# Loads of y ahead of the last output gate, at the joint of attention and merge

## The chip, the core and the metric

The kernel runs on one core of a Trainium2 chip. The time is the device time of one execution in microseconds; below, every number of the trace is in microseconds from the start of the span unless it says ns.

## The reference

Two layers over 1024 tokens of width 1024, all in float32. In each layer four branches give y_a, y_b, y_c, y_m (gated MLP, sparse attention, forgetting attention, memory attention), each 512 wide and each multiplied by the silu of a projection of its own, the output gate. Then the branches are merged:

```python
y_b = nsa_attention(...) * jax.nn.silu(b_z)
up = jnp.einsum('bsnw,nwd->bsnd', ys, w_br)
gates = jax.nn.sigmoid(jnp.einsum('bsd,dne->bsne', h, w_gate))
merged = jnp.einsum('bsnd,bsnd->bsd', gates, up)
out = merged @ w_o
return x + rms_norm(out, g_post)
```

## The kernel before, in words

Every product in full precision is made of three matmuls: each operand is split into a high part (rounded, on ScalarE, `split` L328 or `weight` L220) and a low part (the rest, on VectorE, or on GpSimd for weights), and `mm3` (L247) multiplies high by high, low by high and high by low (lines 251, 254, 255 of the trace). A projection of one 128-column weight for one half of the tokens (c is 0 or 1, 512 tokens) is 8 x 3 = 24 matmuls into a PSUM bank of the pool pj (two banks).

A layer runs `gates` and `attention`, then `merge`. At the end of `attention` the sparse attention's heads are worked off in units of 256 queries (`nsa_unit` L994): scores (L601, L602), exponentials into tiles p, transposes into PSUM (pt, L633; the compressed part's from tiles pc), their eviction and split on ScalarE and VectorE (L331, L333), and the products with the values (o, L641, L645). `head_out` (L648) then adds the parts in a tile yt on ScalarE and GpSimd and stores it by SP (L657) to od, 64 rows by 256 tokens at a time. Between the scores, work that has nothing to do with them is planned to fill TensorE; its list FILL ends with gate y4, whose two tiles th are stored for later (L521). The fill follows the scores at a pace: `follow` (L261) ties a matmul to a score matmul by order alone.

`gate_out` (L1208) makes one output gate: for each half, it loads the head pair's output (tile oo, L1215), projects, takes tanh on ScalarE (z, L341) and a step on VectorE (L342), multiplies by oo on GpSimd (L1217) and stores y (L1218). The last one, bz of head pair 3 in branch 1, is the first thing in `merge`, since it needs the last head.

`add_branch` (L1300) goes over the branches in the order 0, 2, 3, 1. `get_y` (L1310) loads the branch's four tiles yf for each half and splits them into yh and yl. A unit (`gated` L1320) is then 12 matmuls into a bank of s (three banks), a tile th with the gate, and a VectorE step into acc. For branch 0 all gates have been stored before, so th is only loaded. Units of branch 0 run e = 0 to 7 and c = 0, 1.

What sets the order: instructions are ordered by a planner with a clock of its own, program order being the priority; each engine, and SP's queue of DMAs, then works in that order. Within a pool, tiles of one tag take turns in its buffers, and `order_slots` (L174) adds this: the first write of a tile waits for the first write of the tile before it of the same tag, to be complete if it is on another engine. The tag st (eight buffers of 2 KB) serves z, oo, yf and th alike. Pools of the attention lie one behind the other in SBUF: pp (p, 12 x 2 KB), qq (queries, 2 x 4), cb (also the pc tiles, 4 x 2), cd (1 KB), yt (3 x 2), and more. In `merge` the pool yh (5 x 8 KB) begins where pp began, and acc0 and acc1 (16 KB each) follow it; a tile can be written as soon as the tiles under it are done with.

Of the kernel before, what the change touches and what calls it, by code (L numbers as in the profile page):

```python
# [213 lines left out]
class Net:  # L214
# [993 lines left out]
    def gate_out(self, n, name, p):  # L1208
# [3 lines left out]
        for c in range(2):  # L1212
# [4 lines left out]
            nc.gpsimd.tensor_mul(z, z, o)  # L1217
            nc.sync.dma_start(self.y[n][p, :, cs], z)  # L1218

    def gate_early(self, n, e):  # L1220

        w = self.a_form(f"g{n}{e}")
        for c in range(2):
            t = self.st("th")
            self.gate_store(n, e, c, t, self.proj(w, c))
# [51 lines left out]
    def merge(self):  # L1277
        nc, tc, a, l = self.nc, self.tc, self.a, self.l
        p = lambda n, b: tc.tile_pool(name=n, bufs=b, reuse_waits="tile")
        with p("yh", 5) as self.pyh:  # L1280
            with p("acc", 1) as pacc:
                self.acc = [pacc.tile([128, 8, 512], F32, name=f"acc{c}") for c in range(2)]
                self.gate_out(1, "bz", 3)
                for n in (0, 2, 3, 1):
                    self.add_branch(n)
            gp = self.pyh.tile([128, 1024], F32, name="gp", tag="yh")
            nc.sync.dma_start(gp, a["g_post"][l].partition_broadcast(128))
            self.early = "banks"
            with p("kf", 4) as self.pkk, p("vf", 3) as self.pvv, p("tf", 1) as self.ptp:
                self.out_proj(0, gp)  # L1290
                if l + 1 < self.depth:
                    self.mem_norm(l + 1)
                self.out_proj(1, gp)
                if l + 1 < self.depth:
                    self.l, self.xsrc = l + 1, self.x1
                    self.fresh()
                    self.mem_kv()
                    self.prenorm()

    def add_branch(self, n):  # L1300
        yy = [self.get_y(n, c) for c in range(2)]
        for cs in ((0, 1),) if n != 1 else ((0,), (1,)):
            for e in range(8):
                wg = None if (n, e, 0) in self.ready else self.a_form(f"g{n}{e}")
                if e % 2 == 0:
                    wu = [z.rearrange("p (e w c) -> p e w c", e=2, w=4) for z in self.weight(f"u{n}{e // 2}")]
                for c in cs:
                    self.gated(n, e, c, wg, [z[:, e % 2] for z in wu], yy[c])
# [154 lines left out]
```

## Time and profile before

| | us |
|---|---|
| median of 3 runs (3148.03 to 3160.84) | 3156.19 |
| the profiled execution | 3157.73 |
| its span, first to last instruction | 3155.9 |
| TensorE busy | 3047.0 (97%) |
| VectorE busy | 1884.3 (60%) |
| ScalarE busy | 1487.9 (47%) |
| GpSimd busy | 1439.2 (46%) |
| mean granted clock of TensorE, as a share of 2.4 GHz | 0.989 |

In the views PE is TensorE, PEld its weight load, DVE VectorE, ACT ScalarE, POOL GpSimd, SP the queue that issues DMAs. Matmuls are pipelined: the duration of one is longer than its distance to the next. "x" counts instructions; "<-" names what ended an idle time.

### The profile page before, as it was taken

What the parts mean: (1) busy time and instruction counts of PE and PEld (TensorE: products, weight loads), DVE (VectorE), ACT (ScalarE), POOL (GpSimd) and SP (SyncE); (2) the same over time, 40 slices, a digit from 0 to 9 for tenths busy, and PEclk for the clock granted to TensorE, in tenths of its full rate; (3) what the DMA queues carried; (4) which work ended last, traced back from release to release, by engine and by line L of the source; (5) the groups of instructions that cost most, each with busy time, mean ns of one, the idle gap of its engine ahead of it and who ended that gap; (6) DMA issues with size and microseconds to landing.
All of it is one profiled execution on the core that took longest, in us unless ns stands there. A gap on an engine that the chain in (4) does not pass through costs nothing.

```text
span 3155.9 us, 45143 instructions
## 1 busy us (share of the span) xinstructions
PE 3047.0 (97%) x15168; PEld 2548.8 (81%) x15168; DVE 1884.3 (60%) x4313; ACT 1487.9 (47%) x3313; POOL 1439.2 (46%) x1142
## 2 busy tenths in 40 slices
PE   7999999999999999899999999999999999998998
PEld 6778878888888888688787788788878888886887
DVE  7555447868667855336474653578785678553363
ACT  5433345566556654323353433455655566552132
POOL 6844534543233322258577445355432333232684
PEclk9999999999999999999999999999999999998999
DMA  6544495564234322456665345855632342324564
GB/s 221 153 134 132 140 276 158 177 191 125 84 108 146 106 94 94 139 174 195 205 201 177 104 130 162 251 164 180 200 104 83 113 146 96 105 89 149 171 197 147
DMA packets 251673, 475.15 MB, mean 151 GB/s; under 512 B 42513, under 2 KB 96785, under 8 KB 251441
## 3 DMA queue, kind: packets, MB, share of 16 engines
q1 hardware_dynamic: 251440, 472.26, 47.6%
q8 instruction: 120, 1.97, 0.3%
q14 instruction: 113, 0.92, 0.1%
HBM read 334.73 MB, written 137.43 MB: 150 GB/s over the span
## 4 chain that ended last, share of the span: by engine, by line
PE 82%; DVE 5%; DMA 4%; POOL 3%; issue 2%; ACT 2%; SPq 1%; DVEq 0%; POOLq 0%; ACTq 0%
PE pj L251 11%; PE pj L254 11%; PE pj L255 11%; PE s L481 5%; PE s L301 5%; PE s L254 5%; PE o L645 5%; PE s L251 5%; PE s L255 5%; PE pt L633 5%; PE pj L481 4%; PE pj L301 4%; PE s L601 3%; PE s L602 3%; DVE p L674 1%
## 5 line engine op out<-in xcount | busy, mean ns | idle before, releaser
L229 POOL TENSOR_TENSOR wl<-wr,wh 128x1024 fp32r<-128x1024 f32 (+1 forms) x232 | 527.4, 2275 | 609.9 <-ACT wh L227 535.0
L251 PE MATMUL pj<-hh,wh 128*128 128x512 f32 x1648 | 651.5, 395 | 2.4 <-DVE z L342 1.8
L255 PE MATMUL pj<-hh,wl 128*128 128x512 f32 x1648 | 652.3, 396 | 0.0
L254 PE MATMUL pj<-hl,wh 128*128 128x512 f32 x1648 | 650.5, 395 | 0.0
L227 ACT ACTIVATE wh<-wr 128x1024 fp32r<-128x1024 f32 x232 | 245.5, 1058 | 341.1 <-PE s L254 86.7
L611 ACT ACTIVATE p<-p,nm 128x384 f32<-128x384 f32 (+3 forms) x512 | 306.8, 601 | 203.5 <-DVE nm L606 200.4
L333 DVE TENSOR_TENSOR pt<-pt,pt 128x512 fp32r<-128x512 f32 (+1 forms) x464 | 291.9, 635 | 134.8 <-ACT pt L331 133.4
L251 PEld LDWEIGHTS pj<-hh,wh 128*128 128x128 f32 x1648 | 310.9, 189 | 61.0 <-DVE z L342 2.7
L255 PEld LDWEIGHTS pj<-hh,wl 128*128 128x128 f32 x1648 | 310.6, 188 | 59.2
L254 PEld LDWEIGHTS pj<-hl,wh 128*128 128x128 f32 x1648 | 310.6, 188 | 58.0
L331 ACT ACTIVATE pt<-pt 128x512 fp32r<-128x512 f32 (+1 forms) x464 | 251.7, 554 | 212.5 <-PE pt L633 154.3
L645 PE MATMUL o<-pt,v 128*128 128x512 f32 (+1 forms) x864 | 245.1, 371 | 8.8 <-DVE pt L333 8.5
L654 POOL TENSOR_TENSOR yt<-yt 128x256 f32<-128x256 f32 x128 | 100.1, 782 | 300.9 <-ACT yt L653 241.0
L633 PE MATMUL pt<-ident,p 128*128 128x128 f32 x1488 | 230.6, 272 | 0.7 <-DVE pt L333 0.5
L251 PE MATMUL s<-yh,wh 128*128 128x512 f32 x512 | 201.1, 396 | 24.7 <-ACT yh L331 24.7
L633 PEld LDWEIGHTS pt<-ident,p 128*128 128x128 f32 x1488 | 184.9, 140 | 43.0 <-DVE pt L333 0.7
L254 PE MATMUL s<-yl,wh 128*128 128x512 f32 x512 | 201.4, 393 | 0.8 <-DVE yl L335 0.8
L255 PE MATMUL s<-yh,wl 128*128 128x512 f32 x512 | 200.7, 392 | 0.0
L601 PE MATMUL s<-kd,q 128*128 128x512 f32 (+2 forms) x512 | 187.4, 369 | 13.2 <-DVE nm L606 13.2
L602 PE MATMUL s<-kl,q 128*128 128x512 f32 (+2 forms) x512 | 175.5, 344 | 0.0
L645 PEld LDWEIGHTS o<-pt,v 128*128 128x128 f32 x864 | 147.6, 188 | 33.4 <-DVE pt L333 13.6
L676 DVE TENSOR_SCALAR p<-p,r,sg 128x384 f32<-128x384 f32 (+2 forms) x320 | 165.9, 574 | 1.7
(379 smaller groups left out, 6577.4 us busy)
## 6 DMA issues: line engine op xcount, KB each, us to landing
wr<-wt SPq DMA_DIRECT2D x250, 512.0 KB
th<-thd SPq DMA_DIRECT2D x124, 256.0 KB
thd<-gu SPq DMA_DIRECT2D x72, 256.0 KB
q<-rq SPq DMA_DIRECT2D x32, 512.0 KB
yf<-y SPq DMA_DIRECT2D x64, 256.0 KB
thd<-th SPq DMA_DIRECT2D x52, 256.0 KB
vd<-vs SPq DMA_DIRECT2D x48, 256.0 KB
v<-vd SPq DMA_DIRECT2D x24, 512.0 KB
```

Source lines behind the costliest of these rows:

```text
L229: nc.gpsimd.tensor_sub(lo[:, :n], raw[:, :n], hi.bitcast(F32)[:, :n])
L251: ins = nc.tensor.matmul(out, ah, bh, start=k == 0, stop=False)
L254: nc.tensor.matmul(out, ah, bl, start=False, stop=False)
L255: nc.tensor.matmul(out, al, bh, start=False, stop=k == n - 1)
L301: self.nc.tensor.matmul(ps[i], a[:, kk, ts], b[:, k], start=kk == n == 0, stop=kk == 7 and n == 2)
L333: (nc.gpsimd if pool else nc.vector).tensor_sub(lo, src, hi.bitcast(F32))
L481: nc.tensor.matmul(out, w[a][:, k], t[b][:, k], start=start and k == x == 0, stop=k == 3 and x == 2, skip_group_check=True)
L601: self.mark(nc.tensor.matmul(ps[:, :w], q[:, tq], kd[:, b0:b0 + w], start=True, stop=False), 1 + n / 128)
L602: nc.tensor.matmul(ps[:, :w], q[:, tq], kl[:, b0:b0 + w], start=False, stop=True)
L611: nc.scalar.activation(p[:, :n], p[:, :n], AF.Exp, bias=init, scale=-1.0, accum_out=l[:, x:x + 1])
L633: nc.tensor.transpose(pt[:, off + x * 128:off + x * 128 + 128], src, self.ident)
L645: nc.tensor.matmul(o[:, :, t0:t0 + m], it["v"], w[:, :, off:off + m], start=first, stop=last)
```

## The change

`gate_out` of the last gate is taken out of `merge` and cut in two. `gate_begin` loads and splits the weight, projects both halves and makes both z; it stands in `add_branch` of branch 0 behind the loads of y, and while it is traced the pace is set so that its projections come behind the last score matmul in TensorE's order. `gate_end` loads both oo, multiplies and stores; it stands ahead of e = 2 of branch 0, so behind four units.

```diff
+    def gate_begin(self, name, p):
+        w = self.a_form(f"{name}{p}")
+        zz = []
+        for c in range(2):
+            z = self.st("z")
+            self.silu2(z, self.proj(w, c))
+            zz.append(z)
+        return zz
+
+    def gate_end(self, n, p, zz):
+        for c, z in enumerate(zz):
+            cs = slice(c * 512, c * 512 + 512)
+            o = self.st("oo")
+            self.nc.sync.dma_start(o, self.od[n][p, :, cs])
+            self.nc.gpsimd.tensor_mul(z, z, o)
+            self.nc.sync.dma_start(self.y[n][p, :, cs], z)
...
                 self.acc = [pacc.tile([128, 8, 512], F32, name=f"acc{c}") for c in range(2)]
-                self.gate_out(1, "bz", 3)
                 for n in (0, 2, 3, 1):
                     self.add_branch(n)
...
         yy = [self.get_y(n, c) for c in range(2)]
+        if n == 0:
+            self.pace = (1, 1, 1, 0.0)
+            gated = self.gate_begin("bz", 3)
+            self.pace = None
         for cs in ((0, 1),) if n != 1 else ((0,), (1,)):
             for e in range(8):
+                if n == 0 and e == 2:
+                    self.gate_end(1, 3, gated)
```

## Rows read from the trace of the kernel before

**Rows 1.** The page: busy time by engine, and the chain's shares by engine.
```profile
PE 3047.0 (97%) x15168; PEld 2548.8 (81%) x15168; DVE 1884.3 (60%) x4313; ACT 1487.9 (47%) x3313; POOL 1439.2 (46%) x1142
...
PE 82%; DVE 5%; DMA 4%; POOL 3%; issue 2%; ACT 2%; SPq 1%; DVEq 0%; POOLq 0%; ACTq 0%
```

**Rows 2.** Waits of TensorE, 1270 to 1330: us in total, times, longest.
```profile
PE s L251 <- ACT yh L331: 12.1, 1, 12.1
PE o L645 <- DVE pt L333: 2.4, 5, 0.6
```

**Rows 3.** Waits of TensorE, 2838 to 2910.
```profile
PE s L251 <- ACT yh L331: 12.6, 1, 12.6
```

**Rows 4.** Windows, first layer: length, busy by engine (instructions), PEclk, DMA share, GB/s.
```profile
1263.50:1279.20 15.70, 15.69 (x79) 12.82 (x77) 7.35 (x21) 7.20 (x17) 4.07 (x4) 1.00 0.23 71
1279.20:1289.90 10.70, 8.27 (x46) 5.99 (x46) 5.50 (x9) 5.82 (x11) 5.52 (x5) 1.00 0.26 80
1289.90:1302.00 12.10, 0.01 (x1) 0.00 (x0) 0.69 (x2) 2.24 (x4) 2.70 (x3) 0.67 0.32 99
1302.00:1307.80 5.80, 5.78 (x13) 4.28 (x14) 4.30 (x7) 4.01 (x7) 0.00 (x0) 0.52 1.01 350
1307.80:1345.00 37.20, 37.20 (x165) 30.78 (x165) 10.68 (x16) 6.11 (x8) 7.18 (x3) 1.00 0.56 177
```

**Rows 5.** Windows, second layer: the gap and the stretch behind it.
```profile
2859.24:2871.85 12.61, 0.00 (x2) 0.00 (x1) 0.71 (x2) 2.26 (x5) 2.70 (x3) 0.56 0.30 97
2871.85:2877.82 5.97, 5.97 (x14) 4.42 (x14) 4.44 (x7) 4.10 (x7) 0.00 (x0) 0.51 1.02 350
```

**Rows 6.** The chain that ended last, 1292 to 1303: start, us, what.
```profile
1292.67 1.92 DMA o<-yt
1294.64 2.69 DMA oo<-o
1297.36 0.61 ACT z L341
1297.98 3.33 DMA yf<-y
1301.34 0.64 ACT yh L331
1302.02 0.79 PE s L251
```

**Rows 7.** Timeline of SP: start, us, instruction, count.
```profile
1266.34 0.32 SPq L521 DMA_DIRECT2D thd<-th  x1
...
1285.96 7.16 SPq L657 DMA_DIRECT2D o<-yt  x2
...
1297.98 2.22 SPq L1316 DMA_DIRECT2D yf<-y  x5
```

**Rows 8.** Timeline of TensorE: projections, last scores, last transposes of pc and p.
```profile
1257.01 0.50 PE L251 MATMUL pj<-hh,wh 128*128 128x512 f32 x1 [0.88 <-DVE z L342]
...
1263.12 0.34 PE L602 MATMUL s<-kl,q 128*128 128x384 f32 x1
...
1278.79 0.40 PE L255 MATMUL pj<-hh,wl 128*128 128x512 f32 x1
...
1281.09 0.27 PE L633 MATMUL pt<-ident,pc 128*128 128x128 f32 x1
...
1287.63 0.49 PE L633 MATMUL pt<-ident,p 128*128 128x128 f32 x3
```

**Rows 9.** Instructions on the tile yf: ns min/median/max, first and last start.
```profile
L335 DVE SCALAR_TENSOR_TENSOR yl<-yf,yh x64: 677/691/2859, 1302.0 to 3022.4; 128x512 fp32r<-128x512 f32 x64
```

**Rows 10.** Timeline of GpSimd in the last head's stretch.
```profile
1280.43 2.37 POOL L229 TENSOR_TENSOR wl<-wr,wh 128x1024 fp32r<-128x1024 f32 x1
```

**Rows 11.** Timelines of VectorE and GpSimd, later in the first merge.
```profile
1350.68 2.79 DVE L335 SCALAR_TENSOR_TENSOR yl<-yf,yh 128x512 fp32r<-128x512 f32 x2
...
1349.61 2.71 POOL L229 TENSOR_TENSOR wl<-wr,wh 128x1024 fp32r<-128x1024 f32 x1 [8.54 <-ACT wh L227]
```

## The prediction

> **What bounds the kernel now.** I read the page's busy shares and its chain first. TensorE is busy 97% of the span and 82% of the chain runs over it [rows 1]: work taken off another engine is worth nothing by itself, and only microseconds in which TensorE stands still, or runs at the lower clock, can be won. So the next view is TensorE's waits around the two places that the diff touches, the joints between attention and merge. The last head's second half ends on TensorE at 1289.9 us in the first layer and 2859.2 us in the second, and the first matmul of the merge, waiting for the split of a y tile, starts 12.1 and 12.6 us later [rows 2, 3]. No other single wait in the first of them is over 0.6 us [rows 2].
>
> The windows show the rest of the loss. Before the gap the granted clock is 1.00 (2.4 GHz); in the gap it falls to 0.67 and 0.56 as a mean, and in the 5.8 and 6.0 us behind it, it is 0.52 and 0.51, which is the lower level, 1.2 GHz [rows 4, 5]. Only 13 and 14 matmuls run in these two stretches. At the pace of the stretch that follows (165 in 37.20 us, 0.225 us each [rows 4]) they would take 2.9 and 3.2 us. So the lower clock and the waits for splits in it cost 2.9 us in the first layer and 2.8 in the second. The gap and its cold tail together: 12.1 + 2.9 + 12.6 + 2.8 = 30.4 us, 1.0% of the time.
>
> What fills the gap is in the chain, in order of time [rows 6]: the last store of the last head's output takes 1.92 us, the load of its half tile for the output gate (oo) 2.69, the tanh of the gate's projection (z) 0.61, and only then the first y load 3.33, its split 0.64, the first matmul of the merge. The tanh needs nothing from oo, and the y loads of branch 0 need nothing from the gate of head pair 3: y[0] was finished long before. They stand in this order because all of them take tiles of the tag st, and the first write of each such tile waits for the first write of the one before it in the program. SP's own list shows the same: the y loads go out right behind that tanh, at 1297.98 [rows 7].
>
> **The change part by part.**
>
> Moved: the 16 y loads (8 in each layer) now come ahead of the gate's z and oo in the program. The st tiles before them are the two th of y4, whose second store goes out at 1266.34 [rows 7]. With eight buffers and eight loads the last one can go when that store has read its tile, about 2 us later by the 1.92 us of the chain's store. Five of these loads were issued in 2.22 us [rows 7], so eight take 3.6; the first landed after 3.33 [rows 6], and their 2.1 MB at the 350 GB/s of the busy stretch [rows 4] take 6 us, where the DMA share is now only 0.23 to 0.26. So from 1268.3 all y tiles are in SBUF by about 1278, before the last head ends. SP passes eight more entries ahead of the head's stores; this delays a store by 3.6 us at most, and no store is on TensorE's path any more.
>
> The splits of y then need their destinations. The five 8 KB buffers of yh lie on three pieces of pp, one of qq and one of cb. qq is free after the last scores (1263.12), cb when the last transpose of a pc tile is through (1281.09), and the last p tile is read at 1287.63 [rows 8]. So the pair of half c=0 can be written from about 1281.4 on if the planner takes qq and cb, and at the worst from 1288.1, still 1.8 us before the last matmul of the head. A split takes 0.64 us on ScalarE and 0.69 on VectorE [rows 6, 9], and a unit of the merge uses one pair per three matmuls, 0.68 us: one split ahead of TensorE is enough.
>
> Held back: the 48 projection matmuls of bz3. In the trace the last scores run at 1263.12 and the projections behind them are still those of y4 [rows 8]: 72 projection matmuls run from 1257.01 to 1278.79, the first 24, to 1264.5, for y4's second half, the other 48 for bz3. Those already stand behind the last scores, so this order takes away nothing that was used. I price it at 0; it would cost up to 48 x 0.225 = 10.8 us per layer if these matmuls had filled holes before the scores, but the stretch behind the scores is full either way (15.69 of 15.70 us busy [rows 4]). The two banks of pj stay occupied until the z's are read; branch 0 has all its gates stored and asks for no pj, so nobody waits.
>
> Moved later: two oo loads, two multiplications on POOL, two stores of y[1], now ahead of the fifth unit of branch 0. Branch 1 is the last that reads them. POOL is busy 7.18 of the 37.20 us there [rows 4], and TensorE waits for none of it. 0.
>
> What is late next. The merge's first DVE result goes to acc0, which lies on the buffers of yt: it must wait for the head's last store, which lands at 1294.6 [rows 6]. TensorE has three banks of s, three units of 12 matmuls or 8.1 us, before it needs that; starting at 1289.9 it gets to 1298. The th loads wait, by the same rule of order, for the second z; a load like oo's takes 2.69 us, so z must be done by about 1294. Both covers are some 3 us.
>
> What is left to pay is crowding. In the stretch of the last head (10.70 us) VectorE is busy 5.50 [rows 4]; eight splits and one more z step of 0.69 add 6.2, 11.7 in all: 1.0 us too much. Beside it POOL subtracts a weight for 2.37 us [rows 10], and a pair of splits beside such a subtraction took 2.79 us instead of 1.38 [rows 11]: 1.4 more. So the price is between a gain of 2.4 us a layer (the holes of the last head, 10.70 less 8.27 [rows 4], filled with merge matmuls that come early) and a loss of 2.4. I take 1.5 lost, near the upper of the two: the head's own splits and these share in-order queues. The sum: 30.4 less 2 x 1.5 = 27.4 us.
>
> One rule speaks against the change. The row first: POOL's 2.71 us subtraction at 1349.61 and the two y splits at 1350.68 that end after it [rows 11]. The Trainium skill, SBUF — State Buffer, section Who interferes with whom, says that a VectorE instruction with two SBUF inputs and a GpSimd instruction that reads SBUF exclude each other for a whole instruction. By it every POOL step in the last head's stretch would hold up a split, also the small yt additions, for which no row of this trace has a split beside them; the sum would be that of the first rival below.
>
> The profiled execution took 3157.7 us (span 3155.9), 1.5 above the median of the runs, 3156.2. 3157.7 - 27.4 = 3130.3; on the scale of the median 3128.8, so 3129.
>
> **The rivals.**
>
> Crowding at its full size. The splits and z's stand in the queues of ScalarE and VectorE between the last head's evictions. That head waits already for its evictions (five waits, 2.4 us [rows 2]). For: POOL is busy 5.52 us in that stretch [rows 4], and a split beside a POOL step has waited for it [rows 11]. Against: TensorE has merge matmuls to run meanwhile, and the small steps may fall between the splits. If all of the 5.52 falls on the path, 30.4 - 2 x 5.5 = 19.4 is won: 3137.
>
> The loads don't come early. SP issues in order; if the planner puts the y loads behind the last head's two stores, they go out at about 1293.1, land 3.3 us later, and with 0.64 for the split TensorE starts at 1297.1: 4.9 us a layer won, the clock still lost. 3156.2 - 9.8 = 3146, no change by measure. For: the planner issues by its own clock, and two stores stand there for 7.16 us [rows 7]. Against: the loads' tiles are free 17 us earlier.
>
> Slower. The planner puts ScalarE's first y splits ahead of the last head's evictions, and in the run their load or destination is late. Then evictions, PV matmuls and merge all stand behind one waiting ScalarE instruction, and every microsecond of it is one of TensorE's. The place is ScalarE's queue between 1278 and 1288. The last head's 8.3 us of matmuls [rows 4] then run after that split, so it decides against the change from 1302.0 - 8.3 = 1293.7 on; at 1301.3, where the first split is now [rows 6], all 8.3 us are lost in each layer: 3156.2 + 2 x 8.3 = 3173. Against: nothing that such a split needs is later than 1288.
>
> **How the numbers follow.** Forecast 0.70, crowding 0.14, loads late 0.10, slower 0.06. One measurement can't tell less than about 0.5%, 15.8 us, from no change: faster means below 3140.4. Forecast and crowding lie below it, 0.84; same 0.10; slower 0.06. For the range, the lower end is the full 30.4 with the holes filled, 3156.2 - 30.4 - 4.9 = 3121, less 2 for the spread between runs (3148 to 3161): 3119. The upper end takes in the late loads: 3146.
>
> **What would show it.** TensorE's wait before the first merge matmul shrinks from 12 us to under 2 in both layers; the granted clock stays at 1.00 across the joint and no stretch of some 6 us at 0.5 follows; SP issues the y loads before the last head's stores; the splits start between 1281 and 1289; the last scores and the projections of bz3 stand where they are. Wrong would be: y loads behind the last store (late loads), VectorE full and waits of PV matmuls for evictions that grow by several microseconds (crowding), or a ScalarE wait for a y load with evictions queued behind it (slower).

## The result and the profile after

The kernel after takes 3130.53 us (median of 5 runs, 3127.7 to 3137.16); the kernel before, beside it, took 3156.19. The ratio is 0.9921, with an interval of 0.9908 to 0.9935: 0.8% faster. Its profiled execution took 3133.41 us (span 3131.4) against 3157.73: 24.3 us less (the medians differ by 25.7).

TensorE's waits come first, as before [rows 2, 3]: the wait for a y split is 0.5 us where it was 12.1 and 12.6, and a new one has come, for the VectorE step into acc0. The columns are us in total, times, longest. First layer, then second:

```profile
PE s L251 <- DVE acc L1356: 2.4, 1, 2.4
PE o L645 <- DVE pt L333: 1.3, 3, 0.5
...
PE s L251 <- ACT yh L331: 0.5, 1, 0.5
```
```profile
PE s L251 <- DVE acc L1356: 1.9, 1, 1.9
...
PE s L251 <- ACT yh L331: 0.5, 1, 0.5
```

The waits for evictions in the last head (o, L645) fell too, from five with 2.4 us to three with 1.3. The windows of the first layer (length, busy time of each engine, then granted clock, DMA share, GB/s) answer to [rows 4]: there is no stretch at 0.67 or 0.52 any more. The fourth line is the new wait, at a granted clock of 1.00.

```profile
1265.30:1281.00 15.70, 15.70 (x80) 13.04 (x79) 7.47 (x21) 7.03 (x16) 4.07 (x3) 1.00 0.56 188
1281.00:1289.80 8.80, 7.50 (x44) 5.47 (x43) 4.27 (x8) 5.70 (x11) 4.29 (x4) 1.00 0.22 67
1289.80:1299.25 9.45, 8.97 (x39) 6.98 (x38) 6.78 (x11) 5.94 (x12) 1.48 (x2) 1.00 0.29 94
1299.25:1301.66 2.41, 0.00 (x1) 0.00 (x0) 0.74 (x2) 0.00 (x0) 0.00 (x0) 1.00 0.56 209
1301.66:1345.00 43.34, 43.34 (x191) 35.90 (x192) 17.63 (x25) 9.21 (x12) 13.74 (x7) 1.00 0.70 228
```

SP's list (start, us for all of the group, instruction, count) shows the y loads 29.5 us earlier than in [rows 7], straight behind the store of th. The last head's second store (the second line of L657) goes out at 1296.71, behind three loads of th:

```profile
1268.13 0.32 SPq L521 DMA_DIRECT2D thd<-th  x1
1268.50 3.77 SPq L1340 DMA_DIRECT2D yf<-y  x8
...
1287.05 0.45 SPq L657 DMA_DIRECT2D o<-yt  x1
1295.35 1.28 SPq L1349 DMA_DIRECT2D th<-thd  x3
1296.71 0.45 SPq L657 DMA_DIRECT2D o<-yt  x1
1297.26 0.54 SPq L1349 DMA_DIRECT2D th<-thd  x1
1297.89 3.21 SPq L1235 DMA_DIRECT2D oo<-o  x2
```

ScalarE's list (the bracket is the idle time ahead) says why that store is late. All splits of y stand behind the head's last eviction (1289.22), and L655, which moves the head's half tile for its store, stands behind four splits and a z:

```profile
1289.22 0.49 ACT L331 ACTIVATE pt<-pt 128x384 fp32r<-128x384 f32 x1 [0.93 <-PE pt L633]
1289.60 2.18 ACT L331 ACTIVATE yh<-yf 128x512 fp32r<-128x512 f32 x4
1291.69 0.59 ACT L341 ACTIVATE z<-pj 128x512 f32<-128x512 f32 x1
1292.16 0.59 ACT L653 ACTIVATE yt<-o 128x512 f32<-128x512 f32 x1
1292.64 2.19 ACT L331 ACTIVATE yh<-yf 128x512 fp32r<-128x512 f32 x4
1294.72 0.60 ACT L341 ACTIVATE z<-pj 128x512 f32<-128x512 f32 x1
1295.34 0.42 ACT L655 ACTIVATE yt<-yt 64x256 f32<-64x256 f32 x1
```

GpSimd's list in the same stretch; its 2.21 us of idle time before L656 are a wait for that move:

```profile
1292.89 0.74 POOL L654 TENSOR_TENSOR yt<-yt 128x256 f32<-128x256 f32 x1 [5.87 <-issue]
1295.84 0.74 POOL L656 TENSOR_TENSOR yt<-yt 64x256 f32<-64x256 f32 x1 [2.21 <-ACT yt L655]
```

In the second layer the chain of waits (start, us, what) goes through the store itself, which takes 3.58 us where it took 1.92 [rows 6]:

```profile
2853.83 3.58 DMA o<-yt
2857.53 0.70 DVE acc L1356
2858.27 0.50 PE s L251
```

In the first layer the landing shows on SP's queue. The second load of oo, which reads what this store writes, waits for it (us in total, times, longest) and goes out at 1300.78, as the second of the two in SP's list above. So that store landed some 4.0 us after its issue at 1296.71:

```profile
SPq L1235 <- DMA o<-yt: 2.4, 1, 2.4
```

A measure for one joint alone will be needed, since upstream work varies by microseconds between executions: from the start of the last score matmul (L602) to the start of the eighth VectorE step into acc (after: three from 1300.92 on, the eighth at 1315.60). Before, the first joint is 1326.89 - 1263.12 [rows 8] = 63.77 us; after, 1315.60 - 1264.91 = 50.69. The timelines of VectorE (before, after) and TensorE (after) give the ends:

```profile
1326.89 0.69 DVE L1332 SCALAR_TENSOR_TENSOR acc<-th,s 128x512 f32<-128x512 f32 x1 [2.03 <-PE s L255]
```
```profile
1300.92 1.88 DVE L1356 SCALAR_TENSOR_TENSOR acc<-th,s 128x512 f32<-128x512 f32 x3 [4.34 <-DMA oo<-o]
...
1315.60 0.69 DVE L1356 SCALAR_TENSOR_TENSOR acc<-th,s 128x512 f32<-128x512 f32 x1 [2.04 <-DMA th<-thd]
```
```profile
1264.91 0.34 PE L602 MATMUL s<-kl,q 128*128 128x384 f32 x1
```

In the second layer it is 2896.84 - 2832.35 = 64.49 before and 2872.21 - 2822.02 = 50.19 after. The joints give 13.1 + 14.3 = 27.4 us. The spans differ by 24.5, because the last score of the first layer comes 1.8 us later, the stretch between the joints is 1.0 us longer (1506.4 against 1505.5) and the end 0.1.

### The profile page after: what moved, and what is told of

The parts are those of the page before. It is cut to its first block, busy times and chain, and to the rows that moved or that the text cites. A ratio compares the mean times of both kernels' runs of the same rounds, so it can differ in the third digit from the quotient of the medians.

```text
span 3131.4 us, 45147 instructions
## 1 busy us (share of the span) xinstructions
PE 3045.3 (97%) x15168; PEld 2548.3 (81%) x15168; DVE 1881.5 (60%) x4313; ACT 1486.0 (47%) x3313; POOL 1438.6 (46%) x1142
## 4 chain that ended last, share of the span: by engine, by line
PE 82%; DVE 5%; DMA 4%; POOL 4%; ACT 3%; issue 3%; SPq 1%; DVEq 0%; POOLq 0%; ACTq 0%
PE pj L251 11%; PE pj L254 11%; PE pj L255 11%; PE s L481 5%; PE s L301 5%; PE o L645 5%; PE pt L633 5%; PE s L254 5%; PE s L251 4%; PE s L255 4%; PE pj L481 4%; PE pj L301 3%; PE s L601 3%; PE s L602 3%; POOL wl L229 1%
## 5 line engine op out<-in xcount | busy, mean ns | idle before, releaser
L645 PE MATMUL o<-pt,v 128*128 128x512 f32 (+1 forms) x864 | 244.4, 370 | 6.4 <-DVE pt L333 6.2
L654 POOL TENSOR_TENSOR yt<-yt 128x256 f32<-128x256 f32 x128 | 100.4, 784 | 302.3 <-ACT yt L653 240.1
L602 PE MATMUL s<-kl,q 128*128 128x512 f32 (+2 forms) x512 | 175.5, 344 | 0.0
L645 PEld LDWEIGHTS o<-pt,v 128*128 128x128 f32 x864 | 147.6, 188 | 30.2 <-DVE pt L333 10.3
```

The lines of the kernel that those rows point to most:

```text
L602: nc.tensor.matmul(ps[:, :w], q[:, tq], kl[:, b0:b0 + w], start=False, stop=True)
L645: nc.tensor.matmul(o[:, :, t0:t0 + m], it["v"], w[:, :, off:off + m], start=first, stop=last)
```

## The experiments

The theory: the change wins because two cuts together take the chain oo, tanh, y load off TensorE's path, and with the hole goes its cold tail. What remains is the store that acc0 waits for. Rivals: the gain is the clock's; or the reordering of one half does it all; or the store isn't what TensorE waits for (in the first layer the bracket at 1300.92 names a load of oo). Each ratio goes by runs of the kernel before made beside that kernel (medians 3155.14 to 3156.19).

| kernel | joint, layer 1 / 2 | median us | ratio to before, interval |
|---|---|---|---|
| before | 63.77 / 64.49 | 3156.19 | |
| after | 50.69 / 50.19 | 3130.53 | 0.9921, 0.9908 to 0.9935 |
| no pace | 52.05 / 52.14 | 3128.45 | 0.9921, 0.9908 to 0.9933 |
| whole gate behind the y loads | 56.59 / 56.07 | 3139.28 | 0.9951, 0.9939 to 0.9964 |
| cut gate ahead of the y loads | 50.19 / 50.43 | 3128.05 | 0.9922, 0.9907 to 0.9936 |
| before, 46 matmuls in the gap | 63.44 / 63.44 | 3154.57 | 0.9999, 0.9988 to 1.0009 |
| before, 58 matmuls in the gap | 63.10 / 63.27 | 3152.41 | 0.9986, 0.9975 to 0.9997 |
| after, yt moved | 47.99 / 48.00 | 3121.19 | 0.9891, 0.9876 to 0.9907 |
| after, store first | 49.25 / 49.27 | 3126.77 | 0.9909, 0.9894 to 0.9925 |
| cut gate first, yt moved | 48.50 / 48.51 | 3120.98 | 0.989, 0.9875 to 0.9906 |
| before, yt moved | 63.60 / 63.33 | 3157.25 | 1.0001, 0.9989 to 1.0012 |

**The halves of the change.** The first kernel leaves out the pace:

```diff
-            self.pace = (1, 1, 1, 0.0)
             gated = self.gate_begin("bz", 3)
-            self.pace = None
```

> The change without its pace: the projections of bz3 are free to go ahead of the last scores. Theory A (the gain is the order of the tiles of st: y loads and z no longer behind oo): 3131 us like the changed kernel, within 5, and the same places of the bz3 projections, 13 or more us behind the last scores' start. Rival C (holding the projections back is what fills the joint): 3140 or more, with a longer wait of TensorE before the first merge matmul.

Its instructions stand in the same order as the change's on every engine, and its ratio is the same. The held-back projections are an empty part: they stood behind the last scores anyway. Its joints are 1.4 and 1.9 us longer than the change's at the same order. In the first, the clock of its profiled execution accounts for that: it fell behind the wait for acc (last section), to a mean of 0.67 over 5 us, which is 1.65 us less work, and the wait is 0.3 us shorter.

The second keeps the y loads first but makes the gate whole behind them:

```diff
-            gated = self.gate_begin("bz", 3)
+            self.gate_out(1, "bz", 3)
...
-                if n == 0 and e == 2:
-                    self.gate_end(1, 3, gated)
```

> The gate is not cut in two: it stands whole (oo, z, product, store) behind the y loads. Theory A: the y loads still go out before the last head ends and the first merge matmul stands within 1 us of the last head's end at the full clock; but z of the second half waits for oo again, and the th loads for that z, so that TensorE runs out of banks of s after three units and waits some 5 us in place of 2.4 and 1.9: 3136 us. Rival B (what counts is that z and all behind it is rid of the oo load): the old joint comes back, 3150 to 3156.

Faster than before by 0.49%, slower than the change. TensorE starts the merge without a long wait and then stands 6.2 and 6.0 us before the fourth unit, where some 5 were expected. The first line is that wait; below it, the chain of waits of this kernel, first layer, shows the old chain with th in the place of y:

```profile
PE s L251 <- DVE acc L1354: 6.2, 1, 6.2
```
```profile
1294.24 1.95 DMA o<-yt
...
1296.34 2.70 DMA oo<-o
...
1299.12 0.61 ACT z L341
...
1299.75 2.60 DMA th<-thd
...
1302.56 0.70 DVE acc L1354
...
1303.31 0.79 PE s L251
```

The third cuts the gate but leaves its first half ahead of the y loads:

```diff
-        yy = [self.get_y(n, c) for c in range(2)]
         if n == 0:
             self.pace = (1, 1, 1, 0.0)
             gated = self.gate_begin("bz", 3)
             self.pace = None
+        yy = [self.get_y(n, c) for c in range(2)]
```

> The other half alone: the gate is cut and oo comes late, but both z stand ahead of the y loads, as before the change. Theory A in its wide form (either half takes oo off the chain): z runs as soon as its projection is done, some 10 us before the last head's end, six y loads follow at once, and the first merge matmul stands within 1 us of the last head's end; the last two y loads wait for a free buffer of st, which costs up to 2 us a layer: 3131 to 3136. Narrow form (the y loads must come ahead of the z): 3145 or more, TensorE waits for a y split for 6 us or more.

This is the whole gain, 0.9922; the up to 2 us a layer that the last two y loads were to cost did not come. The y loads go out later, behind the first tanh and with the last two at 1286.19, which is 26.6 us behind the last score where the change has 3.6 for the first, and still in time:

```profile
1277.01 2.69 SPq L1340 DMA_DIRECT2D yf<-y  x6
...
1286.19 0.92 SPq L1340 DMA_DIRECT2D yf<-y  x2
```

So the two cuts of the theory are not both needed. Cutting the gate, which frees the tanh from the load of oo, is enough for the whole gain; the y loads first, without it, bring 0.49%; and once the gate is cut, the order of y loads and tanh among themselves is worth nothing here.

**The clock.** Two kernels keep the order of before and fill the gap with matmuls whose result nobody reads (46, then 58); `last_pv` is the last of the products with the values (L645):

```diff
...
+                with tc.issue_after(self.last_pv.ins):
+                    junk = self.ps.tile([128, 512], F32, name="s")
+                    for k in range(46):
+                        nc.tensor.matmul(junk, self.ones_r, self.hh[0][:, k % 8, :], start=k == 0, stop=k == 45)
```

> The kernel before, with 46 matmuls more per layer, of data that nobody reads, on TensorE between the last head's end and the first merge matmul: 10.4 us of the 12 us gap are filled, the gap itself stays. It measures the clock's share alone. By the sum of the prediction (2.9 and 2.8 us lost behind the gap at the lower level): granted clock 1.00 behind the joint and 3156 - 5.7 = 3150.5. If the slow matmuls there were slow for the y splits and not for the clock: 3156, unchanged.

The time stayed where it was, but that doesn't price the clock. The 46 left a hole of 1.5 us (first line, TensorE's waits), and the granted clock fell behind it all the same (windows):

```profile
PE s L251 <- ACT yh L331: 1.5, 1, 1.5
```
```profile
1304.00:1306.00 2.00, 2.00 (x7) 1.14 (x7) 1.05 (x2) 0.96 (x2) 0.00 (x0) 0.69 0.88 289
1306.00:1308.00 2.00, 2.00 (x5) 1.28 (x5) 1.39 (x2) 1.29 (x3) 0.00 (x0) 0.50 1.05 404
1308.00:1310.00 2.00, 2.00 (x10) 1.55 (x9) 1.69 (x3) 1.54 (x3) 0.00 (x0) 0.95 1.03 358
```

So the hole was closed with 58:

> The kernel before with 58 idle matmuls in the gap in place of 46, so that no hole is left ahead of the first merge matmul; they end some 0.8 us after it could start. With 46, a hole of 1.5 us was left and the granted clock still fell to 0.5 for 3.4 us behind the gap. If that hole brought it down: the clock stays at 1.00, from the last scores to the eighth step into acc it is 61.8 us in both layers (63.8 and 64.5 without the matmuls, less 2.9 and 2.8, plus 0.8), and the time 3151. If the clock falls because of what runs after the gap (a burst of y splits and loads): it falls here too, 63.5 us, 3155.

Now the clock stays at 1.00 in both layers, so the burst of y splits and loads behind the gap, which is there too, does not bring it down by itself. The windows of the first:

```profile
1300.00:1304.00 4.00, 3.78 (x17) 2.79 (x16) 2.40 (x4) 2.46 (x5) 0.00 (x0) 1.00 0.95 305
1304.00:1308.00 4.00, 3.89 (x18) 2.89 (x17) 3.21 (x6) 2.42 (x4) 0.00 (x0) 1.00 1.01 350
```

From the merge's first matmul to the eighth step into acc this kernel takes 22.9 us, the one before 24.9: of the predicted 2.9 at most 2.0 are the clock's, since the later start also gives the splits a lead. In the second layer it is 22.8 against 25.0. The joint as a whole is only 0.7 and 1.2 us shorter, since the merge itself starts later (40.2 us behind the last score where it was 38.9). The interval says 0.03 to 0.25%. The rival that the clock makes the gain is out: it is a few microseconds of 27.

**What is left.** acc0 lies on the buffers of yt, and so must wait for the head's last store. Moving the pool yt behind tp takes it off them:

```diff
-                    p("yt", 3) as self.pyt, p("kk", nb["kk"]) as self.pkk, \
-                    p("vv", nb["vv"]) as self.pvv, p("tp", 2) as self.ptp:
+                    p("kk", nb["kk"]) as self.pkk, \
+                    p("vv", nb["vv"]) as self.pvv, p("tp", 2) as self.ptp, p("yt", 3) as self.pyt:
```

> The changed kernel with the pool yt moved behind tp, so that acc0 no longer lies on the buffers from which the last head is stored. In the changed kernel TensorE stood 2.4 and 1.9 us for banks of s, because the first step into acc0 waited for that store. If the store is what it waits for: the wait is under 0.5 us in both layers and from the last scores to the eighth step into acc it is 2 us less than 50.7 and 50.2: about 3126 us. If the first th, whose load goes out with three others at the same time, is as late as the store: the wait stays above 1.5 us, 3130 us.

The wait for acc is gone in both layers, and the first step into acc now waits for a load of th. It starts at 1296.49 (VectorE's timeline), 33.1 us behind the last score where it was 36.0, early enough for TensorE. The store itself is still late: SP's second load of oo waits 2.0 us for it, until 1298.86, over 2 us behind that step:

```profile
1296.49 0.69 DVE L1356 SCALAR_TENSOR_TENSOR acc<-th,s 128x512 f32<-128x512 f32 x1 [1.44 <-DMA th<-thd]
```
```profile
SPq L1235 <- DMA o<-yt: 2.0, 1, 2.0
```
```profile
1298.86 0.32 SPq L1235 DMA_DIRECT2D oo<-o  x1
```

The joints are 2.7 and 2.2 us shorter. The other way is to leave acc0 where it is and let the store go first: the second half's splits stand behind the move L655 on ScalarE, the first loads of th behind the store on SP (`last_move` and `last_store` are L655 and L657 of the last head):

```diff
...
-        yy = [self.get_y(n, c) for c in range(2)]
+        if n == 0:
+            yy = [self.get_y(n, 0)]
+            with self.tc.issue_after(self.last_move.ins):
+                yy.append(self.get_y(n, 1))
...
+            if n == 0 and e == 0:
+                with self.tc.issue_after(self.last_store.ins):
+                    nc.sync.dma_start(th, self.thd[self.ready[n, e, c]])
```

> The changed kernel with the last head's store put first: the second half's y splits follow the last move of yt on ScalarE, and the first two th loads follow the last store on SP. Nothing of the memory's layout changes. If the 2.4 and 1.9 us came from that store's place in the two queues (its move behind four splits, its transfer behind three loads of 256 KB): the store lands some 4 us sooner, the wait is under 1 us, and the time 3127 us. If what the first step into acc0 waits for is the th: no less wait than before, 3131 us.

Here too the wait for acc is gone, but the second half's splits are late: the waits for yh grow from 0.5 to 1.4 and 1.5 us, and the joints are 1.4 and 0.9 us shorter than the change's. Both show that the store is what TensorE waited for in the change, the moved pool alone more plainly, since it leaves the store late; the load of oo that the first layer's bracket names only landed beside it.

Last, the same move with the gate cut ahead of the y loads, and alone:

> The kernel with the z ahead of the y loads (gate cut, oo late), and yt moved off acc0 as well. There the wait for banks of s was 1.3 and 1.6 us and the first step into acc0 stood for the last store. Without that: the wait goes, 48.9 us from the last scores to the eighth step into acc, and 3 us less than the z-first kernel, 3125 us. If the last two y loads, which wait for a buffer of st, hold the second half's splits up as long: no gain, 3128.

> The kernel before with the pool yt behind tp and nothing else. With the change, moving yt took 9 us off the median, but only 2.7 and 2.2 us of it lie between the last scores and the eighth step into acc. If the move helps only where the first step into acc0 waits for the last store: no change here, 3156, and 63.8 and 64.5 us at the joints, since the gap there ends with the y loads. If it gains elsewhere, whatever the joint is: 3150 to 3152 with the joints unchanged.

With the cut it ends where the change with it ends (3120.98 and 3121.19; the joints are 1.7 and 1.9 us shorter than those of the cut alone), and alone it is worth nothing: where y comes last, the store has long landed. These two are the fastest versions, 1.1% below before, and beat both kernels.

What stays open: the medians of the change and of the version with yt moved differ by 9.3 us, its joints only by 4.9. The stretch between the joints took 1506.4 us in the change's profiled execution, 1503.7 in the one without pace, which has the same order of instructions, 1501.6 with yt moved and 1501.3 with the cut first and yt moved. No run separates the last two from the spread of single executions.

## Why the prediction was right

**The sum.** 27.4 us were forecast for the two joints, and 27.4 came out at them, 24.3 in the profiled time: 3129 predicted, 3130.53 measured. The mechanism was right, the chain behind the load of oo. But not all of the terms were, and two errors of some 2 us a layer cancel: crowding (1.5 lost forecast, 0.6 gained) and the store (0 forecast, 2.4 and 1.9 lost). That the sum comes out to the tenth is luck. TensorE's losses at the first joint, read the same way in both: before, 12.1 for the gap, 2.9 behind it, 2.4 of waits for evictions, 17.4; after, 2.4 for acc, 1.3 for evictions, 0.5 for a split, 4.2. The difference, 13.2, agrees with the joint's 13.1.

**Gap and tail, 30.4.** Right as the amount that could be won: the gap went, and the clock is 1.00 across the joint. As the price of the clock alone the 2.9 was too large: the kernel with 58 matmuls shows at most 2.0. The step booked the rest to waits for splits; at the full clock a wait of 0.2 us for a split shows there, and no view tells what the other 0.7 are.

**The y loads.** Right: SP issued all eight in 3.77 us (forecast 3.6) from 1268.50 on, 0.4 us behind the store of th. That the forecast says 1268.3 is chance: it let the last load wait 2 us for that store, and this execution runs 1.8 us later. The kernel with the cut ahead showed that far later would have done. The remark that no store is on TensorE's path any more was wrong (see below).

**Where the splits go.** They start at 1289.60, outside the 1281 to 1289 that was named. The last transposes of p run at 1288.69 here, which puts the worst case at 1289.2 in place of 1288.1: the splits are 0.4 us behind it. The planner put them behind the head's last eviction (1289.22). TensorE's timeline shows that the merge's first matmul nevertheless stands ahead of the head's last two products:

```profile
1288.69 0.49 PE L633 MATMUL pt<-ident,p 128*128 128x128 f32 x3
...
1290.28 0.50 PE L251 MATMUL s<-yh,wh 128*128 128x512 f32 x1 [0.48 <-ACT yh L331]
1290.62 0.52 PE L645 MATMUL o<-pt,v 128*128 128x256 f32 x2
```

**Crowding, 1.5 lost per layer.** Wrong in sign. Since the splits stand behind the evictions, they hold none of them up, and the evictions' waits fell by 1.1 us, against 0.5 for the first split. Of the two waits that are gone, one of 0.52 us stood, before, behind a ScalarE tanh that waited for oo (1277.74), and one of 0.58 ahead of the head's last two products, where the merge's first matmul now stands. Nor was much lost to GpSimd, whose 2.37 us subtraction ran at 1281.97, ahead of all these splits. Of the eight splits on VectorE (679/682/869 ns as minimum, median, maximum), the slow one is the first of the group at 1293.31, the one that begins beside GpSimd's L654, 1292.89 to 1293.63:

```profile
L335 DVE SCALAR_TENSOR_TENSOR yl<-yf,yh x8: 679/682/869, 1290.3 to 1295.3; 128x512 fp32r<-128x512 f32 x8
```

That one split, 0.19 us over the median, agrees in kind with the Trainium skill (SBUF — State Buffer, Who interferes with whom: a VectorE instruction with two SBUF inputs and a GpSimd one that reads SBUF shut each other out). Its rival sum of 5.5 us per layer did not come, because hardly any split met a GpSimd step. No run took the GpSimd step away.

**Held-back projections and later oo, 0.** Right: without the pace the order is the same, and no wait for oo or for the multiplications shows on TensorE.

**What is late next, 0.** This step failed. It named the right place (acc0 on the buffers of yt) and the right limit (1298, three banks of s), but took the store's landing from before, 1294.6, and so a cover of 3.4 us. The change itself moved the store: its move L655 fell behind splits and a tanh on ScalarE, so that it was issued at 1296.71 in place of 1292.67, in an execution that runs 1.8 us later, that is 2.2 us late; and with three loads of th just ahead on the same queue it took some 4.0 us (3.58 in the second layer) instead of 1.92. That is 4.3 us. The cover also left out the way from the landing to the fourth unit, 1.0 us with the step into acc (0.7), and the first three units were through 0.5 us sooner than it had them (1299.25, less 1.8). Together 5.8 against 3.4: the fourth unit began 2.4 us late, in the second layer 1.9. Moving yt takes 2.7 and 2.2 us off the joints.

**The rivals.** Crowding at its full size and late loads were not seen, nor the slower case: ScalarE never stood before a y load. One outcome doesn't test the chances.

## What to carry to other kernels

Where tiles of unrelated work share one tag, a chain of waits can follow their order in the program and not the data: look in it for a load that waits for a result it doesn't read, and cut the step whose second half alone needs the late data. Before a cover is booked as safe, place the releasing transfer anew, with what the change puts ahead of it in its engine's and its queue's order; the time that it had before doesn't hold any more. And a tile that is to be written at the seam of two stages should not lie on the buffer that the first stage empties last.

## What the runs showed of the hardware

The granted clock does not follow the length of the hole alone. Behind a hole of 1.5 us (46 matmuls in the gap) it fell to 0.50, 1.2 GHz, for 1.2 + 2.0 + 0.2 = 3.4 us by the three windows above; in the kernel without pace it fell behind holes of 2.1 and 2.3 us, in the window of the first as a mean over hole and tail:

```profile
1295.00:1300.00 5.00, 3.96 (x11) 3.09 (x12) 1.88 (x3) 0.00 (x0) 2.56 (x2) 0.67 0.80 260
```

But in the change's profiled execution, with the same order of instructions, it stayed at 1.00, 2.4 GHz, in and behind a hole of 2.41 us. What decides between them no run here shows.

A 64 KB store took some 4.0 us (first layer) and 3.58 us (second) from issue to landing with three loads of 256 KB issued on the same queue in the 1.4 us before it and two more in the 1.2 us behind it, and 1.92 in the kernel before, with no such load near it. No view here separates the loads ahead from those behind. The window of the change's first layer from the store's issue to the step into acc shows the DMA engines at a share of 0.85, where it was 0.32 in the gap of before [rows 4]:

```profile
1296.70:1300.90 4.20, 2.55 (x12) 1.78 (x10) 0.00 (x0) 0.00 (x0) 0.00 (x0) 1.00 0.85 308
```
